# Feature-wise scale and shift on one core: projections in 4 KB runs, an early store of zeros, the last slab stored whole

## The chip, the cores and the metric

One Trainium2 chip, one core. The metric is the device time of one execution in microseconds (us). Most executions of one kernel agree within 0.3%; some fall into a slower state. The state "slow" is given to a run that is over 1.5% above the fastest of the same kernel. The profile gives a span (first to last instruction), which for these kernels is about 1.8 us below the time.

VectorE is DVE in the profile, GpSimd is POOL, ScalarE is ACT, SyncE is SP, TensorE is PE. An engine name with a q (ACTq, SPq) is its queue of DMA issues. A packet is the piece that one of the 16 DMA engines moves at a time; a turn, below, is the time from the start of one packet of a queue to the start of the queue's next packet on the same engine. Slack is how much later the last store can be issued without the end moving. Where "packet records" are named, the figures come from the packets' own times in the stored trace, not from one of its printed views.

## The reference

```python
def reference(x, conditioning, gamma_proj, beta_proj):   # x: 32 x 512 x 256, float32
    gamma = conditioning @ gamma_proj                    # 32 x 64 @ 64 x 256
    beta = conditioning @ beta_proj
    return (x * (1 + gamma[:, None, :]) + beta[:, None, :]).astype(np.float32)
```

Each of the 32 batches has its own 256 scales and shifts. x is 16.78 MB in and 16.78 MB out; everything else is small.

## The kernel before

x is cut into 4 slabs of 8 batches. A slab is a tile of 128 partitions with 32 rows of 256 values each, so each partition belongs to one batch. The five loads of x are issued by SyncE without waiting for compute (four by 2.1 us, the last at 10.3), and nothing in SBUF is reused. The coefficients are computed once, for all 128 partitions of each slab, by TensorE.

```python
LOADS = {0: [8, 24]}          # slab 0 in two loads, the others whole
GROUP = 16                    # rows per store
ON_DVE = 11                   # of these on VectorE, 5 on GpSimd

nc.scalar.dma_start(out=cond_s, in_=conditioning)
nc.scalar.dma_start(out=gbproj[:, :dim], in_=gamma_proj)      # 64 partitions x 1 KB
nc.scalar.dma_start(out=gbproj[:, dim:], in_=beta_proj)
...                                                           # 5 loads of x on SyncE
for s in range(SLABS):
    p_t = psum.tile([P, 2 * dim], f32, name=f"gb_p{s}")
    nc.tensor.matmul(p_t, lhsT=cond_T[:, s * P : (s + 1) * P], rhs=gbproj,
                     start=True, stop=True)
    ...                                                       # ScalarE copies it to gb_s
for s in range(SLABS):
    ...
    for r0 in range(0, ROWS, GROUP):
        nc.vector.scalar_tensor_tensor(...)                   # v = (gamma + 1) * v
        nc.gpsimd.tensor_tensor(...)                          # w = w * (gamma + 1)
        nc.vector.tensor_add(...)                             # v = v + beta
        nc.gpsimd.tensor_tensor(...)                          # w = w + beta
        nc.scalar.dma_start(out=o_v[s, :, r0 : r0 + GROUP, :],
                            in_=xs[:, r0 : r0 + GROUP, :])    # 2.10 MB
```

## Time and profile before

| | before |
|---|---|
| three recorded runs | 84.39, 85.98, 85.95 us |
| profiled run, its span | 84.35, 82.6 us |
| bytes through the DMA engines | 33.69 MB |
| busiest compute engine | VectorE, 60% |
| beta_proj in SBUF | 14.62 us |
| first large VectorE instruction | 17.52 us |
| last store issued | 66.7 us |

Two of the three recorded runs are 1.8% above the lowest.

The list of DMA issues of the kernel before (size of one, then us from issue to landing) shows how late two tiny loads arrive:

```profile
gbproj<-in_gamma_proj_dram ACTq DMA_DIRECT2D x1, 64.0 KB, 9.1
gbproj<-in_beta_proj_dram ACTq DMA_DIRECT2D x1, 64.0 KB, 12.9
```

Sixty-four KB take 9 and 13 us. This is what the change goes for.

### The profile page before, as it was taken

Reading aid. Unit: us, or ns where it says so; the run is one execution under the profiler, and the core shown is the slowest. Engines: PE = TensorE matmul, PEld = TensorE weight load, DVE = VectorE, ACT = ScalarE, POOL = GpSimd, SP = SyncE. Lnnn points to the kernel's source line nnn. Section 1 sums busy time; section 2 is a strip of 40 time slices with the busy share of each in tenths; the row PEclk is TensorE's granted clock in tenths of the full one; section 3 lists DMA queues with packets and bytes.
Section 4 is the critical chain, followed back from the end, with each engine's and each line's share of the span. In section 5 each row is a group of like instructions: output and inputs, shape, how many; then the busy total and the mean of one; then the engine's idle time right before and its main releaser. Section 6 shows DMA issues by size and latency. Waiting matters only on the chain.

```text
span 82.6 us, 156 instructions
## 1 busy us (share of the span) xinstructions
PE 9.1 (11%) x10; PEld 2.8 (3%) x10; DVE 49.9 (60%) x18; ACT 3.9 (5%) x9; POOL 46.2 (56%) x22
## 2 busy tenths in 40 slices
PE   0080000899600000000000000000000000000000
PEld 0100000443000000000000000000000000000000
DVE  2011000059999999999999999999999920000000
ACT  0600000034400000000000000000000000000000
POOL 2000000069999999999999999999995000000000
DMA  3899999969969989998889979899999999999992
GB/s 56 337 508 397 389 397 524 460 302 508 508 270 492 508 381 381 413 476 381 381 381 556 460 302 460 381 468 421 429 452 389 468 421 421 460 389 452 437 421 87
DMA packets 2080, 33.69 MB, mean 408 GB/s; under 512 B 288, under 2 KB 416, under 8 KB 416
## 3 DMA queue, kind: packets, MB, share of 16 engines
q1 hardware_dynamic: 720, 16.78, 48.6%
q10 hardware_dynamic: 1360, 16.92, 48.0%
HBM read 16.92 MB, written 16.78 MB: 408 GB/s over the span
## 4 chain that ended last, share of the span: by engine, by line
DVE 49%; DMA 16%; issue 11%; PE 2%; ACTq 1%; ACT 1%
DVE xs L100 30%; DVE xs L103 19%; DMA gbproj<-in_beta_proj_dram 16%; PE gb_p L79 2%; ACTq L50 1%; ACTq L48 0%; ACT gb_s L82 0%; ACT gb_s L85 0%
## 5 line engine op out<-in xcount | busy, mean ns | idle before, releaser
L102 POOL TENSOR_TENSOR xs<-xs,gb_s 128x1280 f32<-128x1280 f32 x8 | 23.0, 2895 | 16.2 <-ACT gb_s L82 16.2
L100 DVE SCALAR_TENSOR_TENSOR xs<-gb_p,xs 128x2816 f32<-128x2816 f32 x8 | 24.7, 3083 | 10.9 <-ACT gb_s L85 10.9
L103 DVE TENSOR_TENSOR xs<-xs,gb_p 128x2816 f32<-128x2816 f32 x8 | 24.7, 3086 | 0.3
L104 POOL TENSOR_TENSOR xs<-xs,gb_s 128x1280 f32<-128x1280 f32 x8 | 23.0, 2893 | 0.0
L79 PE MATMUL gb_p<-gbproj,cond_T 64*128 64x512 f32 x8 | 7.2, 1074 | 8.9 <-DMA gbproj<-in_beta_proj_dram 8.9
L74 DVE COPY cond_T<-cond_T_p 64x512 f32<-64x512 f32 x1 | 0.7, 683 | 4.3 <-PE cond_T_p L72 4.3
L79 PEld LDWEIGHTS gb_p<-gbproj,cond_T 64*128 64x128 f32 x8 | 2.5, 328 | 13.7 <-issue 13.7
L72 PE MATMUL cond_T_p<-rident,cond_s 32*64 32x512 f32 x2 | 1.9, 1065 | 3.9 <-DMA cond_s<-in_conditioning_dram 3.9
L82 ACT ACTIVATE gb_s<-gb_p 128x256 f32<-128x256 f32 x4 | 1.5, 383 | 16.4 <-PE gb_p L79 16.4
L85 ACT COPY gb_s<-gb_p 128x256 f32<-128x256 f32 x4 | 1.5, 367 | 0.0
L82 ACT ACT_TABLE_LOAD x1 | 1.3, 1283 | 2.4 <-issue 2.4
L67 DVE COPY rident<-ident 32x512 f32<-32x512 f32 x1 | 0.4, 416 | 1.2 <-POOL ident masks.py:199 1.2
L72 PEld LDWEIGHTS cond_T_p<-rident,cond_s 32*64 32x64 f32 x2 | 0.3, 202 | 3.9 <-issue 3.9
masks.py:197 POOL MEMSET ident<- 32x32 f32 x1 | 0.1, 114 | 0.3 <-POOLq L121 0.3
masks.py:199 POOL TENSOR_SCALAR_AFFINE_SELECT ident<-ident 32x32 f32<-32x32 f32 x1 | 0.2, 202 | 0.1
L121 POOL MEMSET const-float32-0.0<- 128x1 f32 x1 | 0.1, 103 | 0.2 <-issue 0.2
L121 POOL MEMSET const-bfloat16-1.0<- 128x1 bf16 x1 | 0.1, 106 | 0.0
L121 POOL MEMSET const-uint8-127<- 128x1 uint8 x1 | 0.1, 106 | 0.0
L121 POOL MEMSET const-float32-1.0<- 128x1 f32 x1 | 0.1, 103 | 0.0
## 6 DMA issues: line engine op xcount, KB each, us to landing
out_dram<-xs ACTq DMA_DIRECT2D x8, 2048.0 KB, 18.2
xs<-in_x_dram SPq DMA_DIRECT2D x3, 4096.0 KB, 32.9
xs<-in_x_dram SPq DMA_DIRECT2D x1, 3072.0 KB, 12.2
xs<-in_x_dram SPq DMA_DIRECT2D x1, 1024.0 KB, 4.6
gbproj<-in_gamma_proj_dram ACTq DMA_DIRECT2D x1, 64.0 KB, 9.1
gbproj<-in_beta_proj_dram ACTq DMA_DIRECT2D x1, 64.0 KB, 12.9
cond_s<-in_conditioning_dram ACTq DMA_DIRECT2D x1, 8.0 KB, 3.0
```

Of the source, the lines that this page charges most:

```text
L50: nc.scalar.dma_start(out=gbproj[:, :dim], in_=gamma_proj)
L67: nc.vector.tensor_copy(out=rident.rearrange("p (b g) -> p b g", g=REP), in_=ident.to_broadcast([batch, batch, REP]),)
L72: nc.tensor.matmul(cond_T_p, lhsT=cond_s, rhs=rident, start=True, stop=True)
L74: nc.vector.tensor_copy(out=cond_T, in_=cond_T_p)
L79: nc.tensor.matmul(p_t, lhsT=cond_T[:, s * P : (s + 1) * P], rhs=gbproj, start=True, stop=True)
L82: nc.scalar.activation(out=s_t[:, :dim], in_=p_t[:, :dim], func=mybir.ActivationFunctionType.Identity, bias=1.0, scale=1.0)
L85: nc.scalar.copy(out=s_t[:, dim:], in_=p_t[:, dim:])
L100: nc.vector.scalar_tensor_tensor(out=v, in0=rows(g_p, nv), scalar=1.0, in1=v, op0=ALU.add, op1=ALU.mult)
L102: nc.gpsimd.tensor_tensor(out=w, in0=w, in1=rows(g_s, nw), op=ALU.mult)
L103: nc.vector.tensor_add(out=v, in0=v, in1=rows(b_p, nv))
L104: nc.gpsimd.tensor_tensor(out=w, in0=w, in1=rows(b_s, nw), op=ALU.add)
L121: nc = _bacc.Bacc("TRN2", target_bir_lowering=False, num_devices=1)
```

## The change

The intent: get the coefficients earlier by loading the projections in fewer and longer runs (16 partitions with 4 KB each), and pay for it with four accumulated matmuls per half, each over 16 of the 64 conditioning features. A store of zeros of 16 KB is issued early, to rows that a real store overwrites later. The last slab is stored in one piece of 4.19 MB. The main loop is held in program order. The conditioning is now transposed in four pieces and spread by four copies, which the cut below leaves out, as it does the order of the DMA issues (conditioning, zeros, gamma_proj, beta_proj on ScalarE). Cut to its core:

```diff
-    gbproj = consts.tile([cond_dim, 2 * dim], f32)
-    nc.scalar.dma_start(out=gbproj[:, :dim], in_=gamma_proj)
-    nc.scalar.dma_start(out=gbproj[:, dim:], in_=beta_proj)
+    CP = 16
+    CJ = cond_dim // CP
+    gproj_src = gamma_proj.rearrange("(q j) d -> q j d", j=CJ)
+    bproj_src = beta_proj.rearrange("(q j) d -> q j d", j=CJ)
+    warm = consts.tile([16, dim], f32)
+    nc.gpsimd.memset(warm, 0.0)
+    nc.scalar.dma_start(out=slabs[0]["dst"][0:16, 0, :], in_=warm)
...
+    nc.scalar.dma_start(out=gproj, in_=gproj_src)
+    nc.scalar.dma_start(out=bproj, in_=bproj_src)
...
-        nc.tensor.matmul(p_t, lhsT=cond_T[:, s * P : (s + 1) * P], rhs=gbproj,
-                         start=True, stop=True)
+        for half, proj in ((p_t[:, :dim], gproj), (p_t[:, dim:], bproj)):
+            for j in range(CJ):
+                nc.tensor.matmul(half, lhsT=c_t[:, j, :], rhs=proj[:, j, :],
+                                 start=j == 0, stop=j == CJ - 1)
...
+    STORES = [[16, 16], [16, 16], [16, 16], [32]]
```

More of the change, by code (lines that the diff above doesn't have):

```diff
@@ L28 @@
     P = 128
-    SLABS = 4
-    BS = batch // SLABS
-    REP = P // BS
-    ROWS = BS * seq // P
-    assert SLABS * BS == batch and REP * BS == P and ROWS * REP == seq
-    x_v = x.flatten_outer_dims().rearrange("(s p r) d -> s p r d", s=SLABS, p=P)
-    o_v = out.flatten_outer_dims().rearrange("(s p r) d -> s p r d", s=SLABS, p=P)
-    LOADS = {0: [8, 24]}
-    GROUP = 16
-    ON_DVE = 11
+    SLABS = [(8, [8, 24]), (8, [32]), (8, [32]), (8, [32])]
+    assert sum(n for n, _ in SLABS) == batch
+    STORES = [[16, 16], [16, 16], [16, 16], [32]]
+    PIECE, ON_DVE = 16, 11
+    x_f = x.flatten_outer_dims()
+    o_f = out.flatten_outer_dims()
     consts = ctx.enter_context(tc.tile_pool(name="consts", bufs=1))
@@ L44 @@
     psum = ctx.enter_context(tc.tile_pool(name="psum", bufs=1, space=bass.MemoryType.PSUM))
-    cond_s = consts.tile([batch, cond_dim], f32)
-    nc.scalar.dma_start(out=cond_s, in_=conditioning)
-    gbproj = consts.tile([cond_dim, 2 * dim], f32)
-    nc.scalar.dma_start(out=gbproj[:, :dim], in_=gamma_proj)
-    nc.scalar.dma_start(out=gbproj[:, dim:], in_=beta_proj)
-    slabs = []
-    for s in range(SLABS):
-        xs = xpool.tile([P, ROWS, dim], f32, name=f"xs{s}")
-        slabs.append(xs)
-        r = 0
-        for n in LOADS.get(s, [ROWS]):
-            nc.sync.dma_start(out=xs[:, r : r + n, :], in_=x_v[s, :, r : r + n, :])
-            r += n
-        assert r == ROWS
+    slabs = []
@@ new lines, with load @@
+    b0 = 0
+    for s, (n, loads) in enumerate(SLABS):
+        assert P % n == 0
+        rows = n * seq // P
+        r0, r1 = b0 * seq, (b0 + n) * seq
+        slabs.append(dict(
+            n=n, b0=b0, rows=rows, loads=loads,
+            src=x_f[r0:r1, :].rearrange("(p r) d -> p r d", p=P),
+            dst=o_f[r0:r1, :].rearrange("(p r) d -> p r d", p=P),
+            xs=xpool.tile([P, rows, dim], f32, name=f"xs{s}"),
+        ))
+        b0 += n
+    def load(eng, s, i):
+        sl = slabs[s]
+        r = sum(sl["loads"][:i])
+        n = sl["loads"][i]
+        eng.dma_start(out=sl["xs"][:, r : r + n, :], in_=sl["src"][:, r : r + n, :])
@@ new lines @@
+    CP = 16
+    CJ = cond_dim // CP
+    cond_s = consts.tile([batch, cond_dim], f32)
+    gproj = consts.tile([CP, CJ, dim], f32)
+    bproj = consts.tile([CP, CJ, dim], f32)
+    gproj_src = gamma_proj.rearrange("(q j) d -> q j d", j=CJ)
[3 more added lines that the diff above has]
+    nc.scalar.dma_start(out=slabs[0]["dst"][0:16, 0, :], in_=warm)
+    load(nc.sync, 0, 0)
+    nc.scalar.dma_start(out=cond_s, in_=conditioning)
@@ L64 @@
+    load(nc.sync, 0, 1)
+    nc.scalar.dma_start(out=gproj, in_=gproj_src)
+    load(nc.sync, 1, 0)
+    nc.scalar.dma_start(out=bproj, in_=bproj_src)
+    load(nc.sync, 2, 0)
+    load(nc.sync, 3, 0)
     ident = consts.tile([batch, batch], f32)
     make_identity(nc, ident)
-    rident = consts.tile([batch, batch * REP], f32)
-    nc.vector.tensor_copy(
-        out=rident.rearrange("p (b g) -> p b g", g=REP),
-        in_=ident.to_broadcast([batch, batch, REP]),
-    )
-    cond_T_p = psum.tile([cond_dim, batch * REP], f32)
@@ L72 @@
-    nc.tensor.matmul(cond_T_p, lhsT=cond_s, rhs=rident, start=True, stop=True)
-    cond_T = consts.tile([cond_dim, batch * REP], f32)
-    nc.vector.tensor_copy(out=cond_T, in_=cond_T_p)
-    gb_p, gb_s = [], []
-    for s in range(SLABS):
+    gb_p, gb_s = [], []
+    cond_T_p = psum.tile([CP, CJ, batch], f32)
+    for j in range(CJ):
+        nc.tensor.matmul(cond_T_p[:, j, :],
+                         lhsT=cond_s.rearrange("b (q j) -> b j q", j=CJ)[:, j, :],
+                         rhs=ident, start=True, stop=True)
@@ L78 @@
+    for s, sl in enumerate(slabs):
+        n, b0 = sl["n"], sl["b0"]
+        rep = P // n
+        c_t = consts.tile([CP, CJ, P], f32, name=f"cond_T{s}")
+        nc.vector.tensor_copy(
+            out=c_t.rearrange("q j (b g) -> q j b g", g=rep),
+            in_=cond_T_p[:, :, b0 : b0 + n].to_broadcast([CP, CJ, n, rep]),
+        )
         p_t = psum.tile([P, 2 * dim], f32, name=f"gb_p{s}")
-        nc.tensor.matmul(p_t, lhsT=cond_T[:, s * P : (s + 1) * P], rhs=gbproj,
-                         start=True, stop=True)
+        for half, proj in ((p_t[:, :dim], gproj), (p_t[:, dim:], bproj)):
+            for j in range(CJ):
+                nc.tensor.matmul(half, lhsT=c_t[:, j, :], rhs=proj[:, j, :],
+                                 start=j == 0, stop=j == CJ - 1)
@@ L87, with spread @@
         gb_s.append(s_t)
-    def rows(t, n):
+    def spread(t, n):
         return bass.AP(tensor=t.tensor, offset=t.offset, ap=[t.ap[0], [0, n], t.ap[1]])
-    for s in range(SLABS):
-        xs = slabs[s]
-        g_p, b_p = gb_p[s][:, :dim], gb_p[s][:, dim:]
-        g_s, b_s = gb_s[s][:, :dim], gb_s[s][:, dim:]
-        for r0 in range(0, ROWS, GROUP):
-            v = xs[:, r0 : r0 + ON_DVE, :]
-            w = xs[:, r0 + ON_DVE : r0 + GROUP, :]
-            nv, nw = ON_DVE, GROUP - ON_DVE
-            nc.vector.scalar_tensor_tensor(out=v, in0=rows(g_p, nv), scalar=1.0, in1=v,
-                                           op0=ALU.add, op1=ALU.mult)
-            nc.gpsimd.tensor_tensor(out=w, in0=w, in1=rows(g_s, nw), op=ALU.mult)
-            nc.vector.tensor_add(out=v, in0=v, in1=rows(b_p, nv))
-            nc.gpsimd.tensor_tensor(out=w, in0=w, in1=rows(b_s, nw), op=ALU.add)
-            nc.scalar.dma_start(out=o_v[s, :, r0 : r0 + GROUP, :],
-                                in_=xs[:, r0 : r0 + GROUP, :])
+    with tc.manual_schedule():
+        for s, sl in enumerate(slabs):
+            xs = sl["xs"]
+            g_p, b_p = gb_p[s][:, :dim], gb_p[s][:, dim:]
+            g_s, b_s = gb_s[s][:, :dim], gb_s[s][:, dim:]
+            done = 0
+            for n in STORES[s]:
+                for q0 in range(done, done + n, PIECE):
+                    nv, nw = ON_DVE, PIECE - ON_DVE
+                    v = xs[:, q0 : q0 + nv, :]
+                    w = xs[:, q0 + nv : q0 + PIECE, :]
+                    nc.vector.scalar_tensor_tensor(out=v, in0=spread(g_p, nv), scalar=1.0, in1=v,
+                                                   op0=ALU.add, op1=ALU.mult)
+                    nc.gpsimd.tensor_tensor(out=w, in0=w, in1=spread(g_s, nw), op=ALU.mult)
+                    nc.vector.tensor_add(out=v, in0=v, in1=spread(b_p, nv))
+                    nc.gpsimd.tensor_tensor(out=w, in0=w, in1=spread(b_s, nw), op=ALU.add)
+                nc.scalar.dma_start(out=sl["dst"][:, done : done + n, :],
+                                    in_=xs[:, done : done + n, :])
+                done += n
+            assert done == sl["rows"]
 _INS = ['x', 'conditioning', 'gamma_proj', 'beta_proj']
```

## The prediction

> **What bounds the kernel now.** I read the head of the page first, then the packing of the DMA row, then the stretches, then the chain and the timeline of the first 30 us.
>
> The page of the kernel before; the first line gives busy time and share of each engine, the DMA row is the mean busy share of 16 engines in 40 slices of 2.07 us:
>
> ```profile
> span 82.6 us, 156 instructions
> PE 9.1 (11%) x10; PEld 2.8 (3%) x10; DVE 49.9 (60%) x18; ACT 3.9 (5%) x9; POOL 46.2 (56%) x22
> ...
> DMA  3899999969969989998889979899999999999992
> ...
> HBM read 16.92 MB, written 16.78 MB: 408 GB/s over the span
> ```
>
> No compute engine is above 60%, while the DMA row is high from slice 1 to slice 38. The page charges a packet to the moment where it is recorded, so single slices swing; long stretches say more. From the view of stretches (columns: stretch, length, busy of each engine, clock, DMA share, GB/s):
>
> ```profile
> 8.00:12.00 4.00, 0.00 (x0) 0.00 (x0) 0.00 (x0) 0.00 (x0) 0.00 (x0) 1.00 0.99 406
> ...
> 24.00:40.00 16.00, 0.00 (x0) 0.00 (x0) 15.90 (x6) 0.00 (x0) 16.00 (x6) 1.00 0.97 407
> 40.00:60.00 20.00, 0.00 (x0) 0.00 (x0) 19.89 (x7) 0.00 (x0) 20.00 (x8) 1.00 1.00 431
> 60.00:70.00 10.00, 0.00 (x0) 0.00 (x0) 6.54 (x3) 0.00 (x0) 2.98 (x2) 1.00 1.00 428
> 70.00:76.00 6.00, 0.00 (x0) 0.00 (x0) 0.00 (x0) 0.00 (x0) 0.00 (x0) 1.00 1.02 437
> ```
>
> The share is 0.97 to 1.02 whether only loads run (8 to 12), loads and stores (24 to 40) or only stores (70 to 76). The last vector instruction ends at 66.6 us and the span at 82.6: for the last 16 us nothing but stores runs, at full rate. So the kernel is bound by moving 33.69 MB. The chain of waits names something else:
>
> ```profile
> 1.72 12.90 DMA gbproj<-in_beta_proj_dram
> 14.62 0.14 issue
> 14.76 2.06 PE gb_p L79 x2
> 16.82 0.02 issue
> 16.84 0.38 ACT gb_s L82
> 17.22 0.27 ACT gb_s L85
> 17.49 0.02 issue
> 17.52 3.10 DVE xs L100
> ```
>
> This chain is true for the compute: the coefficients wait for beta_proj until 14.62 us and VectorE starts at 17.52. But the chain follows instructions only and stops at 66.6 us with the last VectorE instruction; the store queued behind it is not in it. Whether an earlier VectorE start shortens the kernel depends on whether the stores wait for VectorE or for the DMA engines. The issues show that:
>
> ```profile
> out_dram<-xs ACTq DMA_DIRECT2D x8, 2048.0 KB, 18.2
> xs<-in_x_dram SPq DMA_DIRECT2D x3, 4096.0 KB, 32.9
> ```
>
> 2048 KB is 2.10 MB, which takes 4.9 us at 428 GB/s, yet a store lands 18.2 us after its issue (15.1 at the least). About 10 us of earlier work always stands in the queues when a store is issued. Compute has that much slack.
>
> **What the Trainium skill says.** First, "DMA: Bandwidth & Descriptors", section "Where 436 GB/s comes from", gives 435.2 GB/s for the 16 ports together; the stretches above, at 428 to 437 from 40 us on, agree, so only some 1.5% is left there. Second, the same page, "Queues, rings and completion order": each DMA engine alternates between the queues with work, one whole packet at a time. The trace agrees: gamma_proj and beta_proj, 64 KB each (0.15 us at full rate), land 9.1 and 12.9 us after their issue. In the trace's records of single packets their 1 KB packets leave one at a time, about 0.95 us apart, each behind a 24 KB packet of x that takes 0.92 us. Third, "TensorE: Matmul & The Clock Gate", section "LDWEIGHTS (loading the stationary operand)": the load's time goes with its columns, not with its contraction rows. The trace agrees: 64 columns 202 ns, 128 columns 328 ns. So cutting the contraction from 64 to 16 rows makes no weight load cheaper. Fourth, the same page, section "What's actually happening": the array leaves its half clock after about 3.4 us of sustained work. The trace doesn't show that: in its 7.2 us of matmuls the weight loads stay 0.855 us apart.
>
> **The change part by part.**
>
> Projections. Before, 64 rows over 16 engines are 4 packets of 1 KB per engine and projection, plus the one that signals completion: 5 turns for gamma, 5 for beta. After, 16 rows of 4 KB are 1 packet plus 1 signal: 2 turns each. The early store adds 1 + 1 turns ahead of gamma on the same queue, as the built order shows (conditioning, zeros, gamma, beta). So 6 turns replace 10. Before, gamma's 5 turns ended at 10.3 us and beta's 5 at 14.6, about 0.9 each. With the same first turn (10.3 less 5 x 0.9 = 5.8) gamma lands at 5.8 + 4 x 0.9 = 9.4 and beta at 11.2; fewer descriptors could bring the first turn forward by a few us.
>
> Matmuls. Before: one matmul of 512 columns per slab, in two passes 0.855 us apart, so 1.7 us. After: 8 matmuls of 256 columns, 16 passes. Half the columns make 0.43 us a pass if the weight load (0.33 us) stays hidden beside the matmul, as it does now: 6.8 us per slab and 27 us in all. Gamma's half (3.4) can start at 9.4 and end before beta's half; that starts at 12.8 and ends at 16.2. Plus 0.65 us of ScalarE as in the chain: VectorE starts at about 16.9, with the earlier first turn at about 14. The gain at this point is therefore only 0.6 to 3.5 us, since TensorE gives back 5 us of what the DMA wins. The later slabs' coefficients come at 6.8 us steps while VectorE needs 12.2 us per slab, so it doesn't wait again. The four copies that spread the conditioning (128 x 4 values on 16 partitions) each resemble the old copy at 0.68 us and run before the projections land. Adding to a bank in place of 4 separate products costs nothing that the trace before prices.
>
> Stores. In the built ScalarE order the first store now stands behind the coefficients of slabs 1 and 2, and the second behind those of slab 3. With 6.8 us per slab after 16.2, these come at about 30 and 37 us, against issues at 25.9 and about 30 before. The loads alone (16.92 MB at 428 GB/s, from 2.2 us) keep the engines busy until 2.2 + 39.5 = 41.7 us. By then stores 1 to 4 are out (37.5 and about 40 for the third and fourth), which adds 8.4 MB, to 61 us; stores 5 and 6 to 71 us. The whole last slab is issued when VectorE ends, at 64 to 66 us, so 5 us or more before the queue runs dry. No gap.
>
> Packets and bytes. The last slab in 32 KB runs has 8 packets per engine where 16 were. Packet records give 1.213 us for 32 KB and 0.611 for 16 KB: 8 x (2 x 0.611 - 1.213) = 0.07 us saved. The projections save a similar trifle. The zeros add 16 KB, 0.04 us. The sum on the DMA engines is about -0.1 us of 78.6, and these engines set the end. The first load of x is issued at the same moment, so the start stays at about 2 us, and the 1.2 us after the last packet stays too.
>
> **The rivals.** (1) The coefficients are on the path and 1 to 3.5 us come through to the end: the chain speaks for it; the 18.2 us of landing and the shares of 0.97 to 1.02 against it. It would give 81 to 83.5. (2) TensorE becomes the wait: if each weight load is not hidden, a pass is 0.43 + 0.33 = 0.76, a slab 12.1 us, and the second store, behind the fourth slab's coefficients, goes out near 57 us, while loads and first store last only to 46.5. That leaves some 10 us of idle DMA and a time of 92 to 96. Against it: weight loads in the trace are spaced exactly as the matmuls' columns. (3) The small early store takes away a cost of the first write, or the slower of two states: the unprofiled runs were 84.39, 85.98 and 85.95, the profiled one 84.35, so two levels 1.6 us apart exist. If the zeros removed the upper one, the median falls to 84.3. Nothing in the profiled execution shows a stall at the first stores, whose packets take 0.61 us as all others do, and I know no reason why the upper level should go.
>
> **Range and chances.** The engines' work is unchanged within 0.1 us, so each level of the runs should stay: about 84.3 or 85.9. I put the prediction between them, 85.0, with 83.7 to 86.3, which holds both levels, and half a us beyond. Faster by over 2% needs rival 1 or 3: 0.10. Slower needs rival 2 or an effect of the new order: 0.05. Within 2%: 0.85.
>
> **What would show it.** Right: beta_proj lands by about 11 us (not 14.6), VectorE's first large instruction starts between 13.5 and 17, 64 records of gamma and beta matmuls take about 27 us of TensorE, the DMA share stays near 1.0 from 4 us until the end, and the span is 82.3 to 82.8. Wrong: dips in the DMA share between 40 and 60 us (rival 2), a last landing moved forward together with VectorE's end (rival 1), or runs at one level only, over many repeats (rival 3).

## The result

| | before | changed |
|---|---|---|
| median of 6 runs | 84.53 us | 84.58 us |
| lowest | 84.39 us | 84.48 us |
| slow runs among the 6 | 85.98, 85.95 | 87.02, 87.69 |
| span of the profiled run | 82.6 us | 82.7 us |
| ratio of fast runs (95% interval) | 1 | 1.0007 (0.999 to 1.0024) |

A ratio is the mean time of one kernel's fast runs over the mean of the other's fast runs of the same rounds, so it is not quite the ratio of the medians. The two kernels are equally fast, to 0.25%.

The page of the changed kernel, with the lines that the prediction showed of the kernel before:

```profile
span 82.7 us, 281 instructions
## 1 busy us (share of the span) xinstructions
PE 28.2 (34%) x72; PEld 21.5 (26%) x72; DVE 51.3 (62%) x20; ACT 3.9 (5%) x9; POOL 46.8 (57%) x23
...
DMA  2899969998999699699998899999999999999890
...
HBM read 16.92 MB, written 16.79 MB: 408 GB/s over the span
```

TensorE works three times as long as before (28.2 us against 9.1). The DMA row and the 408 GB/s are as they were. The stretches of the changed kernel (stretch, length, busy of PE, PEld, DVE, ACT, POOL, clock, DMA share, GB/s) say that the DMA engines have no more gaps and no fewer:

```profile
24.00:40.00 16.00, 13.56 (x32) 10.00 (x31) 15.89 (x7) 1.88 (x6) 15.76 (x6) 1.00 1.02 442
40.00:60.00 20.00, 0.00 (x0) 0.00 (x0) 19.90 (x7) 0.00 (x0) 19.76 (x8) 1.00 0.98 421
60.00:70.00 10.00, 0.00 (x0) 0.00 (x0) 6.83 (x3) 0.00 (x0) 4.16 (x2) 1.00 1.03 441
70.00:76.00 6.00, 0.00 (x0) 0.00 (x0) 0.00 (x0) 0.00 (x0) 0.00 (x0) 1.00 1.02 440
```

The issues of the changed kernel:

```profile
out_dram<-xs ACTq DMA_DIRECT2D x6, 2048.0 KB, 18.1
out_dram<-xs ACTq DMA_DIRECT2D x1, 4096.0 KB, 14.9
...
gproj<-in_gamma_proj_dram ACTq DMA_DIRECT2D x1, 64.0 KB, 8.1
bproj<-in_beta_proj_dram ACTq DMA_DIRECT2D x1, 64.0 KB, 10.2
```

The projections land 1.0 and 2.7 us sooner after their issue. Stores still take 18.1 us from issue to landing, so their queue is as full as before. The chain of waits of the changed kernel, at the same place as the one shown in the prediction (start, length, what):

```profile
1.65 8.13 DMA gproj<-in_gamma_proj_dram
9.78 0.14 issue
9.92 7.17 PE gb_p L105 x16
17.09 0.02 issue
17.11 0.38 ACT gb_s L108
17.50 0.27 ACT gb_s L111
17.77 0.02 issue
17.79 3.10 DVE xs L129
```

The wait for data ends at 9.78 us instead of 14.62, 4.84 us sooner. The matmuls between it and ScalarE then take 7.17 us instead of 2.06, which is 5.11 more. VectorE therefore starts at 17.79 us instead of 17.52: the gain in the DMA is given back on TensorE, and 0.27 us more. (The wait is for gamma_proj here and for beta_proj before; beta_proj now lands at about 12.3 us, before its matmuls start at 13.46.)

So there are two reasons why the time could stay: the start of VectorE didn't move, or it would not have mattered. The experiments separate these.

### The profile page after: what moved, and what is told of

The parts are those of the page before. It is cut to its first block, busy times and chain, and to the rows that moved or that the text cites. A ratio compares the mean times of both kernels' runs of the same rounds, so it can differ in the third digit from the quotient of the medians.

```text
span 82.7 us, 281 instructions
## 1 busy us (share of the span) xinstructions
PE 28.2 (34%) x72; PEld 21.5 (26%) x72; DVE 51.3 (62%) x20; ACT 3.9 (5%) x9; POOL 46.8 (57%) x23
## 3 DMA queue, kind: packets, MB, share of 16 engines
q1 hardware_dynamic: 720, 16.78, 48.6%
## 4 chain that ended last, share of the span: by engine, by line
DVE 48%; issue 12%; DMA 10%; PE 9%; ACT 1%; POOL 0%; ACTq 0%; POOLq 0%
DVE xs L129 30%; DVE xs L132 19%; DMA gproj<-in_gamma_proj_dram 10%; PE gb_p L105 9%; ACT gb_s L108 0%; ACT gb_s L111 0%; ACTq L75 0%; POOL ident masks.py:199 0%; POOL ident masks.py:197 0%; POOL warm L74 0%; POOLq L152 0%
## 5 line engine op out<-in xcount | busy, mean ns | idle before, releaser
L105 PE MATMUL gb_p<-gproj,cond_T 16*128 16x256 f32 x32 | 14.6, 633 | 5.2 <-DMA gproj<-in_gamma_proj_dram 5.2
L105 PE MATMUL gb_p<-bproj,cond_T 16*128 16x256 f32 x32 | 14.5, 629 | 0.0
L105 PEld LDWEIGHTS gb_p<-gproj,cond_T 16*128 16x128 f32 x32 | 10.5, 330 | 8.2 <-issue 5.4
L105 PEld LDWEIGHTS gb_p<-bproj,cond_T 16*128 16x128 f32 x32 | 10.6, 332 | 3.0
L98 DVE COPY cond_T<-cond_T_p 16x512 f32<-16x512 f32 x4 | 2.5, 671 | 4.7 <-PE cond_T_p L91 4.7
L91 PE MATMUL cond_T_p<-ident,cond_s 32*16 32x32 f32 x8 | 0.6, 232 | 4.1 <-DMA cond_s<-in_conditioning_dram 4.1
## 6 DMA issues: line engine op xcount, KB each, us to landing
out_dram<-xs ACTq DMA_DIRECT2D x6, 2048.0 KB, 18.1
out_dram<-xs ACTq DMA_DIRECT2D x1, 4096.0 KB, 14.9
```

The source lines that it names most:

```text
L91: nc.tensor.matmul(cond_T_p[:, j, :], lhsT=cond_s.rearrange("b (q j) -> b j q", j=CJ)[:, j, :], rhs=ident, start=True, stop=True)
L98: nc.vector.tensor_copy(out=c_t.rearrange("q j (b g) -> q j b g", g=rep), in_=cond_T_p[:, :, b0 : b0 + n].to_broadcast([CP, CJ, n, rep]),)
L105: nc.tensor.matmul(half, lhsT=c_t[:, j, :], rhs=proj[:, j, :], start=j == 0, stop=j == CJ - 1)
```

## The experiments

"Kernel before" is always the reference of the ratio.

### Is the start of VectorE on the path? (const_coefs)

```diff
-    ...                               # ident, rident, cond_T: the conditioning is not transposed
     for s in range(SLABS):
         p_t = psum.tile([P, 2 * dim], f32, name=f"gb_p{s}")
-        nc.tensor.matmul(p_t, ...)
+        nc.vector.memset(p_t, 0.5)
         s_t = consts.tile([P, 2 * dim], f32, name=f"gb_s{s}")
-        nc.scalar.activation(...); nc.scalar.copy(...)
+        nc.vector.memset(s_t, 0.5)
```

> The kernel before with constants of 0.5 in place of all coefficients (wrong result on purpose; the three small loads stay). VectorE then waits only for the second load of x and starts at about 13.4 us, 4.1 us before the 17.5 of the kernel before. Theory (the DMA engines set the end, compute has slack): span 82.6 +- 0.3, time 84.4, ratio 0.995 to 1.005, the last stores only wait longer in the queue. Rival (the coefficients are on the path, as the chain of waits says): span about 78.5, ratio about 0.95.

Measured: 84.36 us, ratio 0.9987 (0.9961 to 1.0012), span 82.7 us. The result is wrong. The timeline of this run (start, length, engine, what, and the idle time before it with what ended it) shows that VectorE now waits only for x:

```profile
13.96 3.09 DVE L84 SCALAR_TENSOR_TENSOR xs<-gb_p,xs 128x2816 f32<-128x2816 f32 x1 [8.46 <-DMA xs<-in_x_dram]
...
51.53 3.09 DVE L84 SCALAR_TENSOR_TENSOR xs<-gb_p,xs 128x2816 f32<-128x2816 f32 x1 [0.73 <-DMA xs<-in_x_dram]
```

VectorE starts 3.56 us sooner than in the kernel before (4.1 were expected), and none of it reaches the end. The second line shows where part of it went at once: the last slab of x lands later (its last packet ends at 50.5 us, against 48.6 in the kernel before, by the packet records), since the earlier stores now share the DMA engines with it (with the stores issued later, in before_delay5 below, it ends at 42.2), and VectorE waits for it until 51.53 us. The rest is time in the queue: a store lands 21.4 us after its issue, against 18.2. The rival that has the coefficients on the path is out.

### How much slack does compute have? (before_delay2, before_delay5, after_delay2)

The edit, in the kernel before with 2 or 5 additions, and in the changed kernel with 2:

```diff
+    scratch = consts.tile([P, ON_DVE, dim], f32)
+    nc.vector.memset(scratch, 0.0)
+    with tc.manual_schedule():
+        for _ in range(2):            # or 5
+            nc.vector.tensor_add(out=scratch, in0=scratch, in1=rows(gb_p[0][:, dim:], ON_DVE))
         for s in range(SLABS):
             ...                       # the loop as it was, in program order
```

> The kernel before with two additions on VectorE over a scratch tile (3.09 us each, 6.2 us) ahead of its first large instruction, the loop held in program order. Last store issued at about 66.7 + 6.2 = 72.9. Theory: that store's packets begin at about 81.4 - 8 x 0.611 = 76.5 in the kernel before, and an issue comes about 1.4 us ahead of its first packet, so there are some 8 us of slack: span 82.6 +- 0.3, ratio 0.995 to 1.005. Rival (compute on the path): span 88.8, ratio 1.07.

Measured: ratio 0.9999 (0.9962 to 1.0035), span 82.8 us. VectorE's first instruction on x starts at 23.73 us and the last store is issued at 72.9, both 6.2 us later, for nothing.

> As the run with two additions, but five: 15.5 us, beyond the slack of some 8 us. Theory: the queue runs dry and the span grows by about 15.5 - 8.3 = 7.2, to about 90 us, ratio about 1.085. Rival (compute on the path with no slack): span 98, ratio 1.18. If the DMA engines had more slack than reckoned, less than 7.

Measured: ratio 1.0784 (1.0737 to 1.0832), span 89.4 us, 6.8 above 82.6. In the trace the last store is issued at 82.4 us, 15.7 later than in the kernel before (0.2 more than the five additions, as beta_proj landed that much later). The slack of the kernel before is thus 15.7 - 6.8 = 8.9 us. Now the queue does run dry, and the stretches of this run and its list of issues show what that looks like:

```profile
60.00:70.00 10.00, 0.00 (x0) 0.00 (x0) 9.93 (x5) 0.00 (x0) 4.07 (x2) 1.00 0.83 354
70.00:80.00 10.00, 0.00 (x0) 0.00 (x0) 9.93 (x5) 0.00 (x0) 0.00 (x0) 1.00 0.80 341
...
out_dram<-xs ACTq DMA_DIRECT2D x8, 2048.0 KB, 6.2
```

With compute as the bound, the DMA share falls to 0.80 (a store of 4.9 us for every 6.1 us of VectorE) and a store lands 6.2 us after its issue, since nothing stands before it. Beside these lines, the shares of 1.0 and the 18 us of the two kernels are plain to read. The slack can be read off there too: the last store of the kernel before lands 15.1 us after its issue, 8.9 more than these 6.2.

> The changed kernel with the same two additions (6.2 us). Here the last store is the whole slab, issued at 66.9, and its packets begin at 81.5 - 8 x 1.213 = 71.8 (the trace has 71.45), so the slack is only some 3 us where the kernel before has 8. Theory: the span grows by 6.2 - 3.1 = 3.1, to about 85.8, ratio about 1.035 against the kernel before. Rival (storing the last slab whole leaves the slack as it was): span 82.7, ratio 1.00.

Measured: ratio 1.0243 (1.0219 to 1.0268), span 84.8 us, 2.1 above the 82.7 of the changed kernel. The last store is issued at 72.9 instead of 66.9, so the slack of the changed kernel is 6.0 - 2.1 = 3.9 us; its last store lands 14.9 us after its issue in the changed kernel and 11.0 here, which gives the same 3.9. I had reckoned 3.1, taking an issue to be 1.4 us ahead of its first packet. In the packet records of this run the last store, issued at 72.9, has its first packet at 73.8, 0.9 us later, which accounts for 0.5 of the 0.8 us. The gap stands in one stretch of this run:

```profile
68.00:71.00 3.00, 0.00 (x0) 0.00 (x0) 2.96 (x2) 0.00 (x0) 0.00 (x0) 1.00 0.99 426
71.00:74.00 3.00, 0.00 (x0) 0.00 (x0) 1.85 (x1) 0.00 (x0) 0.00 (x0) 1.00 0.43 186
```

The same delay that costs the kernel before nothing costs the changed one 2%. Its last transfer takes 9.8 us instead of 4.9 and can only be issued when the last row is done, so the queue in front of it is empty sooner: the 4.9 us more of last transfer match the 5.0 us less of slack. No run delays the changed kernel with its last slab stored in halves, so this sum, and not a run, puts the loss down to the whole store. The unchanged time hides that the changed kernel has less than half the reserve.

### Do the bytes set the end? (one_store_less)

```diff
-            nc.scalar.dma_start(out=o_v[s, :, r0 : r0 + GROUP, :],
-                                in_=xs[:, r0 : r0 + GROUP, :])
+            if (s, r0) != (0, 0):
+                nc.scalar.dma_start(out=o_v[s, :, r0 : r0 + GROUP, :],
+                                    in_=xs[:, r0 : r0 + GROUP, :])
```

> The kernel before without the first of its eight stores (wrong result on purpose: 2.10 MB of the output are not written). All compute and its times are as before. Theory (bytes set the end): per engine 64 packets of 0.611 us become 56, so 8 x 0.611 = 4.9 us go; the last store is still issued at 66.7 and the queue would run dry only at about 81.4 - 4.9 - 4.9 = 71.6: span 82.6 - 4.9 = 77.7, ratio about 0.942. Rival (a chain of compute sets the end, as the chain of waits draws it): span unchanged, ratio 1.00.

Measured: 79.55 us, ratio 0.942 (0.9396 to 0.9444), span 77.8 us. The result is wrong. VectorE starts at 17.58 us and the last store is issued at 66.7, as in the kernel before, and yet the end comes 4.8 us sooner: 2.3 us per MB. VectorE's start in the chain, and the seven stores with their first and last issue:

```profile
17.58 3.10 DVE xs L100
...
L106 ACTq DMA_DIRECT2D out_dram<-xs x7: 338/339/368, 30.0 to 66.7; - x7
```

### What did each part of the change do? (no_zeros, runs_2k, last_halved, all_whole)

```diff
-    warm = consts.tile([16, dim], f32)
-    nc.gpsimd.memset(warm, 0.0)
-    nc.scalar.dma_start(out=slabs[0]["dst"][0:16, 0, :], in_=warm)
```

> The changed kernel without the early store of zeros. Theory (each packet on the ScalarE queue waits for one packet of x): two turns fewer, so gamma_proj lands some 1.9 us sooner, at about 7.9 (9.8 with the zeros), beta_proj at about 10.4 (12.3), VectorE starts at about 15.9 (17.8); the span stays at 82.7 +- 0.3 and the ratio at 0.997 to 1.003. Rival (the early store does something for the stores that follow): the span grows or the first stores' packets take longer than 0.61 us.

Measured: four runs, 84.52 and 84.33 fast, 87.18 and 87.74 slow; with two fast runs no ratio is given. The span of the fast profile is 82.7 us. The chain of waits of this run:

```profile
1.17 6.69 DMA gproj<-in_gamma_proj_dram
...
7.99 7.17 PE gb_p L102 x16
...
15.87 3.10 DVE xs L126
```

gamma_proj lands at 7.86 us instead of 9.78, so the zeros cost the projections 1.9 us, two turns, and VectorE's start the same 1.9 us. As the store of zeros stood ahead of the projections, it worked against the change's own aim. The end doesn't notice, and the first stores' packets take 0.61 us with and without the zeros.

```diff
-    CP = 16
+    CP = 32
-    warm = ...                        # the three lines of the zeros, as above
```

> As without zeros, but the projections in 2 KB runs on 32 partitions: half the matmuls. Theory: TensorE takes 3.4 us per slab in place of 6.8, 14 us in all; three turns per projection, so gamma_proj at about 8.9 and beta_proj at about 11.8; beta's half needs 1.7 us more and the copies 0.65, so VectorE starts at about 14.3, 3.5 us before the changed kernel. The span stays at 82.6 +- 0.3. Rival: if VectorE's start mattered the span would fall to about 79.

Measured, one look: 84.44 us, span 82.6 us. gamma_proj lands at 8.5 us and beta_proj at 11.6, TensorE is busy for 14.7 us, and VectorE starts at 14.46, 3.3 us before the changed kernel. This is the best start of all versions that compute the right result, and it is worth nothing at the end.

```diff
-    STORES = [[16, 16], [16, 16], [16, 16], [32]]
+    STORES = [[16, 16], [16, 16], [16, 16], [16, 16]]
```

> The changed kernel with the last slab stored in two halves, as before. Theory: only the packets' size differs, 8 x (2 x 0.611 - 1.213) = 0.07 us per engine, so 0.0 to 0.15 us above the changed kernel and within 0.3% of the kernel before. Rival (the whole store loses overlap at the end): 0.5 us or more below the changed kernel.

Measured: fast runs 84.56, 84.58 and 84.70, ratio 1.0023 (1.0008 to 1.0038). Three of six runs were slow (87.12 to 88.54), the profiled one too. Against the changed kernel, whose fast runs were taken in another set (84.48 to 84.62), the difference of about 0.1 us is what was reckoned, but it cannot be told from noise. A loss of 0.5 us by the whole store is ruled out.

```diff
-    STORES = [[16, 16], [16, 16], [16, 16], [32]]
+    STORES = [[32], [32], [32], [32]]
```

> The changed kernel with every slab stored whole, in 32 KB runs. Theory: 32 pairs of packets per engine in place of 8, so some 0.3 us below the kernel with all halves and 0.2 below the changed one: span 82.4 to 82.6, ratio 0.996 to 1.000, no gap in the DMA row. Rival (fewer and later stores let the queue run dry between 40 and 70 us): a span over 84.

Measured: ratio 1.0009 (0.9993 to 1.0025), span 82.7 us, with two slow runs of six (89.17 and 89.76). No gap appeared, but neither did the 0.2 us in the time that fewer packets should save. In the packet records of the two profiles they are there: the packets' times, summed and divided by the 16 engines, are 79.43 us against 79.72 in the changed kernel, and the last data packet ends at 81.29 us against 81.52. But the span ends 1.36 us after that packet, where it was 1.18, and the runs are no faster.

### Can fewer packets make it faster? (whole_loads)

```diff
-    LOADS = {0: [8, 24]}
+    LOADS = {}
...
-            nc.scalar.dma_start(out=o_v[s, :, r0 : r0 + GROUP, :],
-                                in_=xs[:, r0 : r0 + GROUP, :])
+            if s == SLABS - 1:        # only the last slab in halves
+                nc.scalar.dma_start(out=o_v[s, :, r0 : r0 + GROUP, :],
+                                    in_=xs[:, r0 : r0 + GROUP, :])
+        if s < SLABS - 1:
+            nc.scalar.dma_start(out=o_v[s], in_=xs)
```

> The kernel before with slab 0 loaded whole and slabs 0 to 2 stored whole, the last slab in halves (which keeps the larger slack). The small loads now stand behind packets of 32 KB, 1.21 us a turn: beta_proj lands at about 18 (14.6 before) and VectorE starts at about 21 (17.5 before), 3.5 us of the 8.7 us of slack. Theory: fewer packets take 24 x (2 x 0.611 - 1.213) = 0.2 us and the start some 0.2 us off the engines: span 82.2 to 82.6, ratio 0.995 to 1.001. Rival (a later start of VectorE costs): span 86, ratio 1.04.

Measured: 84.75 us, ratio 1.0023 (1.0007 to 1.0039), span 83.0 us. VectorE starts at 21.60 us, 4.1 later than in the kernel before, without the 3.5 us or more of loss that the rival expects. The small gain I expected is not there; it is 0.2% slower instead. The packet records of the two profiles show where it went: the stores' packets take 39.37 us per engine instead of 39.61, the 0.2 us reckoned, but those of the loads take 40.37 instead of 40.14, and the span ends 1.43 us after the last data packet instead of 1.19. Why the loads and the end take longer stays open. No version tried beats the kernel before.

Together:

| kernel | VectorE starts | last store issued | span | ratio of fast runs |
|---|---|---|---|---|
| before | 17.52 | 66.7 | 82.6 | 1 |
| changed | 17.79 | 66.9 | 82.7 | 1.0007 |
| const_coefs | 13.96 | 64.0 | 82.7 | 0.9987 |
| runs_2k | 14.46 | 63.6 | 82.6 | one look |
| no_zeros | 15.87 | 65.0 | 82.7 | too few |
| last_halved | 17.74 | 66.9 | 86.1, a slow profile | 1.0023 |
| all_whole | 17.78 | 66.9 | 82.7 | 1.0009 |
| whole_loads | 21.60 | 70.8 | 83.0 | 1.0023 |
| before_delay2 | 23.73 | 72.9 | 82.8 | 0.9999 |
| after_delay2 | 23.79 | 72.9 | 84.8 | 1.0243 |
| before_delay5 | 33.22 | 82.4 | 89.4 | 1.0784 |
| one_store_less | 17.58 | 66.7 | 77.8 | 0.942 |

Over the eight rows from 13.96 to 23.73 us in which the queue does not run dry, all bytes are moved and the profile is fast, the start moves by 9.8 us and the span by 0.4. Taking away 2.10 MB moves it by 4.8.

## Why the prediction was right or wrong

**The point was wrong, in the step "Range and chances".** There I "put the prediction between" two levels of about 84.3 and 85.9, at 85.0. Against the recorded median of 85.95 this is a forecast of 1.1% faster, and nothing of the sort came: the ratio is 1.0007. It also contradicts my own sum, which gave about -0.1 us. The failing step was to treat the two levels as equally likely ends, in place of starting from the level of the fast runs: no run of the result lies between 84.62 and 85.95, so 85.0 is the time of no run at all. The runs at 85.95 and 85.98 were of the slow state, 1.8% above the fastest; two of the first three recorded runs happened to fall there. In the six runs of the result the median of the kernel before is 84.53. Fast compared with fast, the sum gives 84.39 - 0.1 = 84.3, and the fast runs of the changed kernel are 84.48 to 84.62.

The step's other half, that "each level of the runs should stay", held for the lower level (lowest 84.39 and 84.48) and failed for the upper: the slow runs of the changed kernel are at 87.02 and 87.69, where those of the kernel before are at 85.95 and 85.98. Why is not known, and both lie outside the range of 83.7 to 86.3. The measured 84.58 lies inside it, and "within 2%" at 0.85 was the right call; but that the median fell on the fast level is partly luck, since two of six runs were slow.

**What bounds the kernel: right.** The reading from the shares and the 16 us of stores alone after VectorE's end is shown by one_store_less and const_coefs. The slack read as "about 10 us" from the landing times is 8.9 us by before_delay5: a store alone in the queue takes 6.2 us to land, and not only the 4.9 us of its bytes that I took off.

**Projections: turns right, one size off.** Gamma was to land at 9.4 us and landed at 9.78; beta at 11.2, "by about 11" as a test, and landed at about 12.3. The count of turns is shown by no_zeros, where two turns fewer gave 1.9 us. The turn of 0.9 us was too small for beta: in the packet records the packets of the zeros and gamma start 1.9 us apart for two turns, those of gamma and beta 2.3, and the turn after beta's packet takes 1.5. "Fewer descriptors could bring the first turn forward by a few us" did not happen: the first packet after the conditioning comes at 5.7 us, in the kernel before at 5.6. That the 1 KB packets of the kernel before "leave one at a time" holds for the first six of each engine; the last two of beta_proj leave within one turn, at 12.4 us and after.

**Matmuls: mechanism right, VectorE's start off.** 6.8 us per slab was right: groups of 8 passes follow each other 3.41 us apart (0.43 a pass), after 3.54 for the first. But the step from gamma's landing to ScalarE has the last pass's full length too, 7.17 us, and starts at 9.92. VectorE starts at 17.79, not 16.9, and outside of the 13.5 to 17 that I named as the test. The gain of 0.6 to 3.5 us at this point became a loss of 0.27: both halves of the account were mis-sized by about half a us, in the same direction. For the time it made no difference. The figures that I gave for weight loads (64 columns 202 ns, 128 columns 328 ns) could not tell columns from rows, as the first has 32 rows and the second 64; the changed kernel tells them apart: 16 rows by 128 columns take 332 ns, 64 rows by 128 columns took 334 (medians).

**Stores: right.** The first store was expected at about 30 us and was issued at 30.9, the second at about 37 and was issued at 37.7, each behind coefficients on ScalarE's queue; no gap followed. The fourth, expected at about 40, was issued at 42.5. What I wrote of the whole last slab, that it is issued at 64 to 66 us and "5 us or more before the queue runs dry", was 66.9 us, and 3.9 us by after_delay2. I did not draw the consequence that the change more than halves the reserve.

**Packets and bytes: right in that nothing comes of it.** The 0.1 us saved cannot be seen in the times (by the interval of the ratio, -0.1 to +0.2 us). The same price per packet, applied to all_whole and whole_loads, promised 0.2 us and more; the stores' packets saved it there, and the time did not follow.

**The rivals.** Coefficients on the path: refuted by const_coefs and runs_2k. TensorE as the wait: refuted by the result, since the weight loads stay hidden. Zeros that remove the slow state: refuted by the result, as the changed kernel's own slow runs are at 87.02 and 87.69.

## What to carry to other kernels

Before shortening a chain of waits, see whether the DMA share is near 1.0 after the last compute instruction and how much longer the last store takes from issue to landing than a store that finds the queue empty: both say how much slack compute has, and a start that comes earlier within this slack buys nothing. A change that moves nothing today can still spend the reserve, as the whole last store did, and an added delay is a cheap way to measure that. When the few runs lie on two levels, decide first which are of the same state, and let the forecast of the change start from those.

## What the Trainium skill lacked or had wrong

- "TensorE: Matmul & The Clock Gate", section "What's actually happening": after about 3.4 us of sustained work the array should run at twice its first pace. In the changed kernel float32 passes run back to back for 27 us and never speed up: all 32 matmul records of beta's half are 629 ns, and groups of 8 passes stay 3.41 us apart from the second to the last, after 3.54 for the first. Whether these passes ran at the lower pace throughout, or this data type takes more cycles, no run here tells; nor does the clock column of the views, which reads 1.00 everywhere, as the traces hold no record of the clock.
- "DMA: Bandwidth & Descriptors", section "Anatomy of one DMA — SWDGE (gpsimd) path", gives a fixed cost of about 2.0 us per DMA for the path that GpSimd issues; for those issued by ScalarE and SyncE the page has a time to the first byte and a least round trip, but no cost of a large store from issue to landing. In before_delay5 a store of 2.10 MB that finds the queue empty lands after 6.2 us; less the 4.9 us of its bytes, that is 1.3 us.
- No page that I read has the slow state of a single core. In the one profile that fell into it (last_halved, span 86.1 us) all compute takes as long as ever, and the rate is low while x is loaded, and normal later. The first lines are its stretches, the second those of the changed kernel in the fast state:

```profile
8.00:20.00 12.00, 10.13 (x24) 7.99 (x25) 2.26 (x1) 0.65 (x2) 2.47 (x1) 1.00 0.98 359
20.00:40.00 20.00, 17.51 (x42) 13.09 (x40) 19.86 (x8) 1.94 (x6) 19.69 (x8) 1.00 0.99 382
40.00:52.00 12.00, 0.00 (x0) 0.00 (x0) 11.93 (x5) 0.00 (x0) 11.84 (x5) 1.00 1.01 434
```

```profile
8.00:20.00 12.00, 10.08 (x24) 7.93 (x25) 2.21 (x1) 0.65 (x2) 2.42 (x1) 1.00 1.00 411
20.00:40.00 20.00, 17.56 (x42) 13.14 (x40) 19.86 (x8) 1.94 (x6) 19.69 (x8) 1.00 1.00 433
```

  In the packet records the loads carry all of it: their packets of 32 KB take 1.34 us on average against 1.213 in the changed kernel, and all packets of the loads 43.5 us per engine against 40.2, which is 3.3 of the 3.4 us; those of 16 KB of the stores take 0.611 us in both. The cause is not known; whether other traffic on the chip slows the loads was not tested. On record are 7 slow runs in 35 of the kernel before (85.93 to 86.97 us), 9 in 27 of the changed kernel and its variants (87.02 to 89.76), and none in 22 of the variants of the kernel before; whether some kernels fall into this state more often was not tested.
